# Scores of paired attention steps placed behind the values of the step ahead, and norm roots turned inside the MLP's second block

## The chip, the cores and the metric

The kernel runs on 1 core of one Trainium2 chip. The metric is the device time of an execution in microseconds, the median of the runs shown. TensorE (PE) does the matrix products, VectorE (DVE), ScalarE (ACT) and GpSimd (POOL) the rest, and SyncE (SP) issues most transfers.

## The reference

A trunk of two layers runs over 512 latent tokens and 256 context tokens, 1024 features each, in fp32. A layer is: modulated RMSNorm, one input projection whose columns go to four head groups, the groups, an output projection with a gated residual, a second modulated RMSNorm, and an MLP with squared ReLU. In the second layer the context feeds keys and values alone. What the change touches are two of the head groups and the second norm:

```python
def neighbourhood_attention(p_lat, p_ctx, rpb, need_ctx):
    ...
    s = jnp.einsum('brnqhd,brnkhd->brnhqk', qb, kb).astype(jnp.float32) * scale + bias.astype(jnp.float32)
    s = jnp.where(valid[None, None, :, None], s, NEG_INF)
    s_ctx = jnp.einsum('brnqhd,bkhd->brnhqk', qb, kc).astype(jnp.float32) * scale
    p = jax.nn.softmax(jnp.concatenate([s, s_ctx], axis=-1), axis=-1).astype(v.dtype)
    ...
def window_attention(p_lat, p_ctx, sink, ang, need_ctx):
    """Banded GQA: |i - j| <= SWA_WINDOW over latent tokens, plus all context keys and a per-head sink logit."""
    ...
    p = jax.nn.softmax(jnp.concatenate([s, s_ctx, s_sink], axis=-1), axis=-1).astype(v.dtype)
    ...
        h = h + m[5] * sq_relu_mlp(modulate(rmsnorm(h, g_norm2[l]), m[3], m[4]), w_mlp1[l], w_mlp2[l])
        if need_ctx:
            ...
            hc = hc + mc[5] * sq_relu_mlp(modulate(rmsnorm(hc, g_norm2[l]), mc[3], mc[4]), w_mlp1[l], w_mlp2[l])
```

## The kernel before

**Products.** Activations lie with features on the partitions and tokens along the row. A product of two fp32 operands is done as three products of a narrower type: each operand is split into a high and a low part (`split_w`, ScalarE's cast on L238 and VectorE's difference on L239 for weights), and `dense` (L246 to L263) runs, for one block of 128 output features, 8 products high by high, 8 low by high and 8 high by low into one PSUM bank, for the latent columns (512 wide) and then the context columns (256 wide). Its `evac` takes the result out of the bank. `dense` has a hook, `midway`, a function that is called at the middle product.

**Attention.** `attend` (L387 to L483) does one step: 128 queries of two heads. Its scores (L418 where the two heads are `paired`, L431 where not) go to PSUM banks of the pool `ps_s` (4 banks). Then VectorE takes the row maximum (L441, or L449 to L453 in steps over context keys alone), ScalarE the exponential with its sum (L455, and L458 for the sink), VectorE adds the sink (L459), takes the reciprocal (L460) and normalises (L462). TensorE transposes the probabilities (L473) into banks of the pool `ps_t` (4 banks), `evac` copies them out (ScalarE L374 or VectorE L376), and TensorE multiplies them with the values (L479). The last value product of a step is appended to the list `anchors`. In the paired branch the score products of both heads alternate and are chained by `tc.issue_after`, so that they keep that order; the first of them has no such tie.

`swa()` (L1113) runs the banded steps: 2 pairs of heads by 6 blocks of queries in layer 0 (4 latent, 2 context) and 2 by 4 in layer 1. `na()` (L1172) runs as many neighbourhood steps. `mla()` uses the unpaired branch.

**What sets the order.** Program order is only a wish here: outside the opening of layer 0, a list scheduler places the instructions of each engine by priorities and its own estimate of times, before the kernel runs. At run time each engine, TensorE too, takes its instructions in that fixed order. `tc.issue_after(x)` makes what is issued in it follow x on its engine. `merge` interleaves several chains of work: in the banded stage the steps of `swa()`, the convolution of the state-space group (`conv`, with a dense block ahead of each and four multiply-adds on VectorE, L805) and, in layer 0, splits of output weights; in the neighbourhood stage the steps of `na()`, the state-space scan and blocks of the output projection. `behind`, which `calls` uses, ties a chain's next piece to the value product two steps back (`LAG = 2`). The products of the modulation of the next use (L172 in `mod_steps`) are small pieces that are laid between.

**The norm ahead of the MLP.** `norm_seg` (L311 to L348) is a generator for one stretch of tokens: squares of 8 feature blocks, `rstd_col` (products with ones, L296, and VectorE's root, L282 to L288), `bcast` (the roots are turned to a row by products with the identity, L308), then 8 modulates (VectorE L339, then ScalarE L342/L343 or L346, and GpSimd or VectorE L347). The last stretch (context in layer 0, the second half of the latent tokens in layer 1) isn't done when the MLP begins: `rest` holds what is left of it. The MLP's first 3 blocks (5 in layer 1, `NAHEAD`) run on the first part of the tokens alone (`up_block`, L1281 to L1284 are ReLU, square and split of its result), and `next(rest)` is called in between, 6 times per block (`PACE`): in block 0 at its middle product (the roots' sums), after block 0 five times (the turn and four modulates), after block 1 the rest.

Of the kernel before, what the change touches and what calls it, by code (L numbers as in the profile page):

```python
# [59 lines left out]
PACE = (6, 6, 6)  # L60
# [31 lines left out]
def kernel(ctx: ExitStack, tc: tile.TileContext, D: dict, out: bass.AP, dbg=None):  # L92
# [4 lines left out]
    PE = nc.tensor  # L97
# [14 lines left out]
    def unit(tag, name, dtype=F32):  # L112
        if tag == "u":
            return up.tile([P, T], dtype, tag="u", name=name)
        return kp.tile([P, 776], dtype, tag=tag, name=name, bufs={"pr": 4, "pT": 3, "q": 4}[tag])

    def pss():
        return ps_s.tile([P, 512], F32, tag="s", name=nm("pS"))

    def pst():  # L120
        return ps_t.tile([P, 512], F32, tag="t", name=nm("pt"))
# [120 lines left out]
    def load_w(src, nk, low=V):  # L242
        raw = wp.tile([P, nk, P], F32, tag="wr", name=nm("wr"))
        nc.sync.dma_start(raw, src)
        return split_w(raw, [P, nk, P], wp, "wh", "wl", low=low)
# [4 lines left out]
    def dense(src, acts, segs, evac, ks=range(KD), w=None, low=V, midway=None):  # L250


        k0, nk = min(ks), max(ks) - min(ks) + 1
        wh, wl = w or load_w(src[:, k0:k0 + nk, :], nk, low)
        for s, c0, n in segs:
            ps = pst()
            mm = [(wh, 0, k) for k in ks] + [(wl, 0, k) for k in ks] + [(wh, 1, k) for k in ks]
            for i, (w, a, k) in enumerate(mm):
                if midway and i == len(mm) // 2:
                    midway()  # L260
                PE.matmul(ps[:, :n], w[:, k - k0, :], acts[k][a][:, c0:c0 + n],  # L261
                          start=i == 0, stop=i == len(mm) - 1)
            evac(s, c0, n, ps[:, :n])  # L263
        return wh, wl
# [104 lines left out]
    def evac(dst, src):  # L369

        turn[0] += turn[1]
        if turn[0] >= 1.0:
            turn[0] -= 1.0
            A.copy(dst, src)  # L374
        else:
            V.tensor_copy(dst, src)  # L376

    anchors = []
# [11 lines left out]
    def attend(q, k, parts, sinks, vt, put, sgn=-1.0, paired=False):  # L390
# [8 lines left out]
        def terms(a):  # L399
            if not isinstance(q[a], tuple):  # L400
                return [(q[a], k[a])]
            return [(q[a][0], k[a][0]), (q[a][1], k[a][0]), (q[a][0], k[a][1])]

        ats = ([], [])
        if paired:


            off, prev = 0, None
            for k0, n, tab in parts:
                if off == 0 or off + n - b0 > 512:  # L410
                    banks, b0 = (pss(), pss()), off
                dst = [banks[a][:, off - b0:off - b0 + n] for a in range(2)]
                nmm = len(terms(0))
                for i in range(nmm):
                    for a in range(2):
                        x, y = terms(a)[i]
                        with (tc.issue_after(prev.ins) if prev else nullcontext()):
                            prev = PE.matmul(dst[a], x, y[:, k0:k0 + n], start=i == 0, stop=i == nmm - 1)  # L418
                for a in range(2):
                    ats[a].append((dst[a], off, n, tab))  # L420
                off += n
        else:
            for a in range(2):
                off = 0
                for k0, n, tab in parts:
                    if off == 0 or off + n - b0 > 512:
                        bank, b0 = pss(), off
                    dst = bank[:, off - b0:off - b0 + n]
                    mm = terms(a)
                    for i, (x, y) in enumerate(mm):  # L430
                        PE.matmul(dst, x, y[:, k0:k0 + n], start=i == 0, stop=i == len(mm) - 1)  # L431
                    ats[a].append((dst, off, n, tab))
                    off += n
# [33 lines left out]
        for a in range(2):  # L467
            pT = unit("pT", nm("pT"))
            for g0 in range(0, nkt, 4):
                n = min(4, nkt - g0)  # L470
# [6 lines left out]
        for t in range(nkt):  # L477
            for a in range(2):
                last_mm = PE.matmul(pv[64 * a:64 * a + 64, :P], vt(a, t), pts[a][:, t * P:(t + 1) * P],  # L479
                                    start=t == 0, stop=t == nkt - 1)  # L480
# [139 lines left out]
    def transition(block, norm, parts):  # L620


        w, before = {}, iter(())
        for pi, part in enumerate(parts):
            order = range(KD) if pi % 2 == 0 else range(KD - 1, -1, -1)
            now = norm(*part, order)
            for i, d in enumerate(order):
                w[d] = block(d, part, w[d] if pi and i < REUSE else None)
                for _ in range(BACK[i]):
                    next(before, None)  # L630
                if i:
                    next(now)
            for _ in before:
                pass
            next(now)
            before = now
        return before

    for l in range(DEPTH):
        last = l == DEPTH - 1  # L640
# [3 lines left out]
        parts = [(0, 0, 256), (0, 256, 256)] if last else full  # L644
# [626 lines left out]
        rest = transition(lambda d, p, w: out_block(d, 1, *p, KB, w), norm2, fine)  # L1271
# [4 lines left out]
        def up_block(qd, f, sg, out=None, w=None, midway=None):  # L1276
            hh, hl = out or (unit("u", nm("hh"), F32R), unit("pT" if f == KD - 1 else "u", nm("hl"), F32R))

            def act(s, c0, n, ps):
                r, r2 = unit("q", nm("r")), unit("pr", nm("r2"))  # L1280
                A.activation(r[:, :n], ps, AF.Relu)  # L1281
                A.activation(hh[:, c0:c0 + n], r[:, :n], AF.Square)
                V.tensor_tensor(r2[:, :n], r[:, :n], r[:, :n], ALU.mult)  # L1283
                V.tensor_tensor(hl[:, c0:c0 + n], r2[:, :n], hh[:, c0:c0 + n].bitcast(F32), ALU.subtract)  # L1284

            w = dense(D["w_mlp1"][l, qd * KD + f], nacts, sg, act, w=w, low=(V, G)[LOWU[l]], midway=midway)
            return (hh, hl), w
# [12 lines left out]
        if not last:  # L1300
            sums, ahead = mod_sums(l + 1), split_ahead(l + 1)
# [3 lines left out]
        for qd in range(4):  # L1305
            hid = []
            if qd == 0:
                ahead = []
                for f in range(NAHEAD[l]):
                    ahead.append(up_block(qd, f, parts[:1], midway=None if f else lambda: next(rest)))  # L1310
                    for _ in range(PACE[l] - (f == 0)):
                        next(rest, None)
                for _ in rest:
                    pass
                for f, (o, w) in enumerate(ahead):
                    hid.append(up_block(qd, f, parts[1:], o, w if len(ahead) < 3 else None)[0])
            while len(hid) < KD:
                hid.append(up_block(qd, len(hid), segs)[0])
                more(MV[0])
            if qd < 3:  # L1320
                for d in range(KD):
                    down_block(qd, d, hid, segs)
                    more(MV[1])
# [12 lines left out]
        rest = transition(lambda d, p, w: down_block(3, d, hid, [p], w), norm1, fine)  # L1336
# [132 lines left out]
```

## Time and profile before

| | |
|---|---|
| median of 3 runs | 1802.9 us (1801.73 to 1808.01) |
| the profiled execution | 1802.71 us, its span 1800.9 us |
| granted TensorE clock, mean | 0.987 of full |
| TensorE busy | 1750.6 us, 97% of the span |
| weight loads (PEld) | 1493.3 us, 83% |
| VectorE busy | 1109.4 us, 62% |
| ScalarE busy | 737.8 us, 41% |
| GpSimd busy | 240.3 us, 13% |

A row of a timeline gives the start of an instruction (or of a run of like ones), its time, its engine, line and operation, output and inputs, and in brackets how long the engine was idle before it and what ended that. Buffer numbers are left out of names in the trace and stand in the orders below: `pS` are scores, `pr` probabilities, `pt` a bank of `ps_t`, `wh`/`wl` the parts of a weight, `ah`/`al` of an activation, `rs` norm roots, `xn`, `r`, `hl` blocks of the MLP. The layers' stages lie so in the span: banded attention 205 to 330 us and 1225 to 1300 us, neighbourhood attention with the state-space scan 330 to 465 us and 1300 to 1412 us, the start of the first MLP at about 500 us.

### The profile page before, as it was taken

The numbers are of one execution on the slowest core, as the hardware profiler recorded it, in microseconds if no ns is written. First come the engines' busy times: TensorE is split into PE (matmuls) and PEld (weight loads), VectorE is DVE, ScalarE is ACT, GpSimd is POOL, SyncE is SP. The second block draws the span as 40 slices with busy tenths as digits, with TensorE's granted clock in tenths as the row PEclk, the third lists the DMA queues.
The fourth block names the chain that finished last, engine by engine and source line by source line (L and its number), as shares of the span: only waits on it lengthen the run. The fifth ranks groups of instructions, "written<-read, shape, count | busy, mean of one in ns | idle before, by whom it ended". The sixth has DMA issues, their size and how long they took to land.

```text
span 1800.9 us, 28892 instructions
## 1 busy us (share of the span) xinstructions
PE 1750.6 (97%) x11170; PEld 1493.3 (83%) x11170; DVE 1109.4 (62%) x2372; ACT 737.8 (41%) x1497; POOL 240.3 (13%) x367
## 2 busy tenths in 40 slices
PE   8999999999989999999999999999989999999998
PEld 7877877777878888888888998688878898888888
DVE  5548458688677566467555674757779563444355
ACT  4347546655353123123123443545544451323244
POOL 0102011234320000000000331101114310000002
PEclk8999999999999999999999999899999999999999
DMA  9440267632635445344444534111333543222333
GB/s 337 138 152 17 67 214 248 214 115 93 211 109 177 136 153 163 109 154 144 155 135 146 173 113 138 35 36 36 120 110 104 199 146 100 94 94 94 106 104 119
DMA packets 86249, 238.94 MB, mean 133 GB/s; under 512 B 9200, under 2 KB 17392, under 8 KB 86112
## 3 DMA queue, kind: packets, MB, share of 16 engines
q1 hardware_dynamic: 74976, 208.57, 35.8%
q0 software_dynamic: 7104, 24.33, 3.8%
q10 hardware_dynamic: 4032, 4.20, 0.7%
q8 instruction: 88, 1.44, 0.3%
q14 instruction: 49, 0.40, 0.1%
HBM read 214.52 MB, written 22.54 MB: 132 GB/s over the span
## 4 chain that ended last, share of the span: by engine, by line
PE 89%; DVE 6%; DMA 2%; ACT 1%; issue 1%; POOL 0%; DVEq 0%; ACTq 0%; POOLq 0%; SPq 0%
PE pt L261 68%; PE pt L479 3%; PE pt L473 3%; PE pS L666 2%; PE pS L431 2%; PE pS L418 2%; PE pt L172 1%; PE pt L666 1%; PE pt L296 1%; PE pt L933 1%; PE pS L1031 1%; DVE pr L441 1%; DVE wl L239 1%; PE pt L864 0%; DMA old<-in_hT_dram 0%
## 5 line engine op out<-in xcount | busy, mean ns | idle before, releaser
L238 ACT CAST wh<-wr 128x1024 fp32r<-128x1024 f32 x206 | 215.9, 1049 | 403.0 <-PE pt L261 291.2
L239 DVE TENSOR_TENSOR wl<-wr,wh 128x1024 fp32r<-128x1024 f32 x206 | 253.9, 1233 | 100.5 <-ACT wh L238 96.0
L261 PE MATMUL pt<-ah,wh 128*128 128x512 f32 (+1 forms) x1304 | 275.0, 352 | 7.1 <-ACT ah L346 3.1
L261 PE MATMUL pt<-al,wh 128*128 128x512 f32 (+1 forms) x1304 | 269.5, 347 | 0.0
L261 PE MATMUL pt<-ah,wl 128*128 128x512 f32 (+1 forms) x1304 | 268.7, 348 | 0.0
L261 PEld LDWEIGHTS pt<-ah,wh 128*128 128x128 f32 x1304 | 213.3, 190 | 48.0 <-ACT ah L346 4.3
L261 PEld LDWEIGHTS pt<-ah,wl 128*128 128x128 f32 x1304 | 215.2, 191 | 31.4 <-issue 0.8
L261 PEld LDWEIGHTS pt<-al,wh 128*128 128x128 f32 x1304 | 212.9, 190 | 31.1 <-issue 2.4
L261 PE MATMUL pt<-hh,wh 128*128 128x256 f32 (+1 forms) x896 | 168.2, 330 | 0.0
L261 PE MATMUL pt<-hl,wh 128*128 128x256 f32 (+1 forms) x896 | 167.0, 329 | 0.0
L261 PE MATMUL pt<-hh,wl 128*128 128x256 f32 (+1 forms) x896 | 166.9, 329 | 0.0
L1291 DVE SCALAR_TENSOR_TENSOR h<-pt,mod,h 128x512 f32<-128x512 f32 (+1 forms) x112 | 66.3, 595 | 153.8 <-PE pt L261 153.6
L261 PEld LDWEIGHTS pt<-hh,wh 128*128 128x128 f32 x896 | 137.6, 189 | 17.7 <-issue 0.6
L261 PEld LDWEIGHTS pt<-hh,wl 128*128 128x128 f32 x896 | 138.0, 190 | 15.4
L261 PEld LDWEIGHTS pt<-hl,wh 128*128 128x128 f32 x896 | 138.1, 190 | 15.0
L208 DVE SCALAR_TENSOR_TENSOR ma<-wm,cact,ma 128x768 f32<-128x768 f32 x112 | 109.9, 1013 | 65.3 <-DMA wm<-in_w_mod_dram 65.2
L1281 ACT ACTIVATE r<-pt 128x512 f32<-128x512 f32 (+1 forms) x101 | 51.4, 509 | 237.1 <-PE pt L261 237.1
L1283 DVE TENSOR_TENSOR r<-r 128x512 f32<-128x512 f32 (+1 forms) x101 | 58.2, 577 | 123.0 <-ACT r L1281 122.9
L322 POOL TENSOR_TENSOR sq<-sq,sq 128x256 f32<-128x256 f32 x66 | 64.7, 980 | 442.9 <-ACT sq L318 442.2
L455 ACT ACTIVATE pr<-pr,m 128x512 f32<-128x512 f32 (+2 forms) x96 | 77.8, 811 | 40.3 <-DVE m L441 38.4
L261 PE MATMUL pt<-oh,wo 128*128 128x256 f32 (+1 forms) x576 | 93.9, 306 | 0.0
L261 PEld LDWEIGHTS pt<-oh,wo 128*128 128x128 f32 x576 | 79.0, 194 | 5.5 <-issue 1.7
(295 smaller groups left out, 2473.5 us busy)
## 6 DMA issues: line engine op xcount, KB each, us to landing
wr<-in_w_mlp_dram SPq DMA_DIRECT2D x154, 512.0 KB, 3.5
wo<-oscr SPq DMA_DIRECT2D x66, 512.0 KB, 4.7
wm<-in_w_mod_dram SPq DMA_DIRECT2D x80, 384.0 KB, 3.6
wr<-in_w_a_dram SPq DMA_DIRECT2D x36, 512.0 KB, 4.1
wm<-in_w_mod_dram SPq DMA_DIRECT2D x32, 512.0 KB, 4.0
wr<-in_w_out_dram SPq DMA_DIRECT2D x16, 512.0 KB, 4.3
oscr<-wh POOLq DMA_DIRECT2D x16, 512.0 KB, 3.7
oscr<-wl POOLq DMA_DIRECT2D x16, 512.0 KB, 5.6
```

Of the source, the lines that this page charges most:

```text
L208: V.scalar_tensor_tensor(a[:, :T], w, cact[:, k, i:i + 1], a[:, :T], ALU.mult, ALU.add)
L238: A.copy(wh, raw)
L239: low.tensor_tensor(wl, raw, wh.bitcast(F32), ALU.subtract)
L261: PE.matmul(ps[:, :n], w[:, k - k0, :], acts[k][a][:, c0:c0 + n], start=i == 0, stop=i == len(mm) - 1)
L322: G.tensor_tensor(sq[0][:, :n], sq[0][:, :n], q[:, :n], ALU.add)
L455: A.activation(pr[:, :off], src, AF.Exp, scale=-1.0 if tabs else sgn, bias=mcol, accum_out=s2[:, a:a + 1])
L473: PE.transpose(pt[:, i * P:(i + 1) * P], probs[a][:, (g0 + i) * P:(g0 + i + 1) * P], ident)
L479: last_mm = PE.matmul(pv[64 * a:64 * a + 64, :P], vt(a, t), pts[a][:, t * P:(t + 1) * P], start=t == 0, stop=t == nkt - 1)
L666: PE.matmul(acc[t], acts[k][a][:, t * P:(t + 1) * P], slabs[pc][w][:, kk, :], start=k == 0 and x == 0, stop=k == KD - 1 and x == 2)
L1281: A.activation(r[:, :n], ps, AF.Relu)
L1283: V.tensor_tensor(r2[:, :n], r[:, :n], r[:, :n], ALU.mult)
L1291: V.scalar_tensor_tensor(h[d][:, c0:c0 + n], ps, mod[:, 40 + d, s:s + 1], h[d][:, c0:c0 + n], ALU.mult, ALU.add)
```

## The change

The first score product of a paired step is now tied behind the last entry of `anchors`, the last value product of the step that was issued ahead. Before, only the later ones were tied to each other. And `midway` is now a pair, the product's number and the function: block 0 calls `next(rest)` at product 12 as before, and no more behind it; block 1 calls it at product 6 in layer 0 and 18 in layer 1, so the roots are turned there; all 8 modulates of the stretch follow, 6 after block 1 and 2 after block 2 (as `PACE` has it).

```diff
--- before.py
+++ after.py
@@ -256,8 +256,8 @@
             ps = pst()
             mm = [(wh, 0, k) for k in ks] + [(wl, 0, k) for k in ks] + [(wh, 1, k) for k in ks]
             for i, (w, a, k) in enumerate(mm):
-                if midway and i == len(mm) // 2:
-                    midway()
+                if midway and i == midway[0]:
+                    midway[1]()
                 PE.matmul(ps[:, :n], w[:, k - k0, :], acts[k][a][:, c0:c0 + n],
                           start=i == 0, stop=i == len(mm) - 1)
             evac(s, c0, n, ps[:, :n])
@@ -405,7 +405,7 @@
         if paired:
 
 
-            off, prev = 0, None
+            off, prev = 0, anchors[-1] if anchors else None
             for k0, n, tab in parts:
                 if off == 0 or off + n - b0 > 512:
                     banks, b0 = (pss(), pss()), off
@@ -414,8 +414,8 @@
                 for i in range(nmm):
                     for a in range(2):
                         x, y = terms(a)[i]
-                        with (tc.issue_after(prev.ins) if prev else nullcontext()):
-                            prev = PE.matmul(dst[a], x, y[:, k0:k0 + n], start=i == 0, stop=i == nmm - 1)
+                        with (tc.issue_after(prev) if prev else nullcontext()):
+                            prev = PE.matmul(dst[a], x, y[:, k0:k0 + n], start=i == 0, stop=i == nmm - 1).ins
                 for a in range(2):
                     ats[a].append((dst[a], off, n, tab))
                 off += n
@@ -1307,8 +1307,9 @@
             if qd == 0:
                 ahead = []
                 for f in range(NAHEAD[l]):
-                    ahead.append(up_block(qd, f, parts[:1], midway=None if f else lambda: next(rest)))
-                    for _ in range(PACE[l] - (f == 0)):
+                    now = (12, (6, 18)[last], None)[min(f, 2)]
+                    ahead.append(up_block(qd, f, parts[:1], midway=now and (now, lambda: next(rest))))
+                    for _ in range(PACE[l] if f else 0):
                         next(rest, None)
                 for _ in rest:
                     pass
```

A scheduler decides where instructions come to stand, so three places of its result follow.

TensorE, layer 0, the first banded step (its probabilities are `pr_2635` and `pr_2645`, its scores `pS_2619`, `pS_2620`, `pS_2627`, `pS_2628`). Before:

```order
L261 MATMUL pt_2561<-al_245,wh_2531 128x256
L261 MATMUL pt_2561<-al_247,wh_2531 128x256
L473 MATMUL pt_2656<-con,pr_2635 128x128 x4
L473 MATMUL pt_2662<-con,pr_2635 128x128
L172 MATMUL pt_2330<-wm_2748,cact 32x512 x2
L172 MATMUL pt_2330<-wm_2750,cact 32x512 x2
L418 MATMUL pS_2780<-oh_1726,nqh_2774 128x384
L418 MATMUL pS_2781<-oh_1726,nqh_2774 128x384
L418 MATMUL pS_2780<-oh_1726,nql_2775 128x384
```

In the change:

```order
L418 MATMUL pS_2627<-oh_1726,nqh_2613 128x256
L418 MATMUL pS_2628<-oh_1726,nqh_2613 128x256
L418 MATMUL pS_2627<-oh_1726,nql_2614 128x256
L418 MATMUL pS_2628<-oh_1726,nql_2614 128x256
L418 MATMUL pS_2627<-ol_1727,nqh_2613 128x256
L418 MATMUL pS_2628<-ol_1727,nqh_2613 128x256
L172 MATMUL pt_2330<-wm_2748,cact 32x512 x2
L172 MATMUL pt_2330<-wm_2750,cact 32x512 x2
L473 MATMUL pt_2656<-con,pr_2635 128x128 x4
L473 MATMUL pt_2662<-con,pr_2635 128x128
L473 MATMUL pt_2666<-con,pr_2645 128x128 x4
L473 MATMUL pt_2672<-con,pr_2645 128x128
```

Before, the transposes of `pr_2635` follow the last products of a dense block (`pt_2561`), and the step's last score stands 57 rows above them, ahead of that block. In the change the step's scores stand behind that block, and between the last of them and the transposes of their own probabilities only two rows of the modulation are left.

VectorE, the softmax of the same step. Before:

```order
L441 ISA pr_2635,m_559_2617<-pS_2619,con,mx_2636 128x384
L441 ISA m_559_2617 128x1
L441 ISA pr_2645,m_559_2617<-pS_2620,con,mx_2646 128x384
L441 ISA m_559_2617 128x1
L239 TENSOR_TENSOR wl_2608<-wr_2605,wh_2607 128x1024
L459 TENSOR_TENSOR s_560_2618<-s_560_2618,e_567_2640 128x1
L460 RECIPROCAL s_560_2618<-s_560_2618 128x1
L462 TENSOR_SCALAR pr_2635<-pr_2635,s_560_2618 128x640
L239 TENSOR_TENSOR wl_2693<-wr_2690,wh_2692 128x1024
L459 TENSOR_TENSOR s_560_2618<-s_560_2618,e_570_2650 128x1
L460 RECIPROCAL s_560_2618<-s_560_2618 128x1
L462 TENSOR_SCALAR pr_2645<-pr_2645,s_560_2618 128x640
```

In the change:

```order
L805 SCALAR_TENSOR_TENSOR acc_2595<-raw_2525,hconv_713,acc_2595 128x772
L441 ISA pr_2645,mx_2646<-pS_2628,zero,nsink_2458 128x256
L441 ISA mx_2646 128x1
L441 ISA pr_2635,m_559_2617<-pS_2619,con,mx_2636 128x384
L441 ISA m_559_2617 128x1
L805 SCALAR_TENSOR_TENSOR acc_2595<-raw_2525,hconv_713,acc_2595 128x772
L441 ISA pr_2645,m_559_2617<-pS_2620,con,mx_2646 128x384
L441 ISA m_559_2617 128x1
L805 SCALAR_TENSOR_TENSOR acc_2595<-raw_2525,hconv_713,acc_2595 128x772
L459 TENSOR_TENSOR s_560_2618<-s_560_2618,e_567_2640 128x1
L805 SCALAR_TENSOR_TENSOR acc_2595<-raw_2525,hconv_713,acc_2595 128x772
L460 RECIPROCAL s_560_2618<-s_560_2618 128x1
```

Before, two splits of weights (L239) stand in the chain. Now four steps of a convolution (L805) stand in it, the last of them ahead of the reciprocal, and the normalise (L462) comes two rows further down.

Layer 0's MLP, TensorE where the roots `rs_6009` are summed (L296) and turned (L308), then VectorE behind it. TensorE before:

```order
L261 MATMUL pt_5991<-al_5660,wh_5987 128x512
L261 MATMUL pt_5991<-al_5662,wh_5987 128x512
L296 MATMUL pt_6004<-ones,sq_5825 128x1 x2
L261 MATMUL pt_5991<-al_5664,wh_5987 128x512
L308 MATMUL pt_6037<-con,rs_6009 128x128 x2
L261 MATMUL pt_6066<-ah_5649,wh_6062 128x512
L261 MATMUL pt_6066<-ah_5651,wh_6062 128x512
```

VectorE before:

```order
L288 SCALAR_TENSOR_TENSOR rs_6009<-rsv_6010,rs_6009 128x2
L1284 TENSOR_TENSOR hl_5984<-r_1322_6032,hh_5983 128x512
L339 SCALAR_TENSOR_TENSOR xn_6040<-h_3902,gsc_96,pt_6037 128x256
L339 SCALAR_TENSOR_TENSOR xn_6045<-h_4019,gsc_96,pt_6037 128x256
L339 SCALAR_TENSOR_TENSOR xn_6049<-h_4131,gsc_96,pt_6037 128x256
L339 SCALAR_TENSOR_TENSOR xn_6053<-h_4239,gsc_96,pt_6037 128x256
```

TensorE in the change, from the last products of the next latent block on:

```order
L261 MATMUL pt_6045<-al_5660,wh_6041 128x512
L261 MATMUL pt_6045<-al_5662,wh_6041 128x512
L261 MATMUL pt_6045<-al_5664,wh_6041 128x512
L308 MATMUL pt_6052<-con,rs_6009 128x128 x2
L261 MATMUL pt_6113<-ah_5649,wh_6109 128x512
L261 MATMUL pt_6113<-ah_5651,wh_6109 128x512
```

VectorE in the change:

```order
L288 SCALAR_TENSOR_TENSOR rs_6009<-rsv_6010,rs_6009 128x2
L1283 TENSOR_TENSOR r_1322_6032<-r_6031 128x512
L239 TENSOR_TENSOR wl_6156<-wr_6153,wh_6155 128x1024
L1284 TENSOR_TENSOR hl_5984<-r_1322_6032,hh_5983 128x512
L1283 TENSOR_TENSOR r_1331_6074<-r_6073 128x512
L339 SCALAR_TENSOR_TENSOR xn_6079<-h_3902,gsc_96,pt_6052 128x256
L339 SCALAR_TENSOR_TENSOR xn_6084<-h_4019,gsc_96,pt_6052 128x256
L339 SCALAR_TENSOR_TENSOR xn_6088<-h_4131,gsc_96,pt_6052 128x256
L239 TENSOR_TENSOR wl_6193<-wr_6190,wh_6192 128x1024
L1284 TENSOR_TENSOR hl_6038<-r_1331_6074,hh_6037 128x512
```

The turn (L308) moves from behind block 0 to behind a whole further block (`pt_6045`), and the context's modulates (L339) from behind the roots to behind `r_1331_6074`, the squared result of that further block.

## Rows read from the trace of the kernel before

**Rows 1.** the page: engines (section 1) and chain of waits (section 4)

```profile
PE 1750.6 (97%) x11170; PEld 1493.3 (83%) x11170; DVE 1109.4 (62%) x2372; ACT 737.8 (41%) x1497; POOL 240.3 (13%) x367
...
PE 89%; DVE 6%; DMA 2%; ACT 1%; issue 1%; POOL 0%; DVEq 0%; ACTq 0%; POOLq 0%; SPq 0%
```

**Rows 2.** TensorE's waits: waited for, us in total, times, longest us

```profile
PE pt L308 <- DVE rs L288: 8.6, 4, 3.0
...
PE pt L473 <- DVE pr L462: 0.4, 1, 0.4
```

**Rows 3.** windows: stages, busy us of each engine, granted clock, DMA share, GB/s

```profile
205.00:330.00 125.00, 121.53 (x835) 95.19 (x831) 82.73 (x190) 68.21 (x149) 17.47 (x40) 1.00 0.59 194
330.00:465.00 135.00, 125.80 (x1022) 101.25 (x1022) 105.14 (x350) 73.03 (x205) 47.38 (x70) 0.99 0.40 134
1225.00:1300.00 75.00, 75.00 (x514) 61.30 (x514) 55.51 (x132) 38.75 (x86) 8.75 (x27) 1.00 0.21 68
1300.00:1412.00 112.00, 103.56 (x904) 89.77 (x901) 88.31 (x293) 51.13 (x133) 30.80 (x46) 0.98 0.42 139
```

**Rows 4.** TensorE's timeline, a banded step: start us, us, what, [idle <-releaser]

```profile
241.34 0.50 PE L418 MATMUL pS<-ol,nqh 64*128 64x256 f32 x2
...
251.81 0.71 PE L473 MATMUL pt<-con,pr 128*128 128x128 f32 x5
252.45 1.06 PE L172 MATMUL pt<-wm,cact 128*32 128x512 f32 x8
```

**Rows 5.** VectorE's timeline of the same step

```profile
241.76 0.48 DVE L441 CUSTOM_DVE_ANT_0 pr<-pS,zero,nsink 128x256 f32<-128x256 f32 x1 [3.60 <-PE pS L418]
...
243.65 1.22 DVE L239 TENSOR_TENSOR wl<-wr,wh 128x1024 fp32r<-128x1024 f32 x1
244.79 0.16 DVE L459 TENSOR_TENSOR s<-s,e 128x1 f32<-128x1 f32 x1
...
245.18 0.55 DVE L462 TENSOR_SCALAR pr<-pr,s 128x640 f32<-128x640 f32 x1
```

**Rows 6.** groups by line and shape, VectorE, 205 to 465 us

```profile
L805 DVE SCALAR_TENSOR_TENSOR acc<-raw,hconv,acc 128x772 f32<-128x772 f32 x24 | 24.4, 1017 | 0.5 <-ACT acc L803 0.4
L239 DVE TENSOR_TENSOR wl<-wr,wh 128x1024 fp32r<-128x1024 f32 x17 | 20.8, 1223 | 14.9 <-ACT wh L238 12.2 <-issue 2.5 <-DMA oscr<-wl 0.2
```

**Rows 7.** ScalarE's timeline of the same step

```profile
243.24 0.83 ACT L455 ACTIVATE pr<-pr,m 128x640 f32<-128x640 f32 x1
```

**Rows 8.** TensorE's timeline, layer 0's first MLP blocks

```profile
512.83 0.50 PE L296 MATMUL pt<-ones,sq 128*128 128x1 f32 x4
...
516.68 0.43 PE L308 MATMUL pt<-con,rs 128*128 128x128 f32 x2 [3.01 <-DVE rs L288]
516.87 3.18 PE L261 MATMUL pt<-ah,wh 128*128 128x512 f32 x8
...
529.47 3.01 PE L261 MATMUL pt<-ah,wh 128*128 128x256 f32 x22
...
538.31 2.00 PE L261 MATMUL pt<-ah,wh 128*128 128x512 f32 x8
```

**Rows 9.** TensorE's timeline, end of the neighbourhood stage of layer 0

```profile
462.17 0.40 PE L308 MATMUL pt<-con,rs 128*128 128x128 f32 x2 [2.73 <-DVE rs L288]
```

**Rows 10.** windows of 4 us behind two waits, columns as in rows 3

```profile
464.00:468.00 4.00, 4.00 (x27) 4.00 (x27) 1.34 (x3) 0.00 (x0) 0.00 (x0) 0.71 0.37 126
516.00:520.00 4.00, 3.32 (x11) 2.64 (x12) 3.89 (x9) 2.23 (x6) 0.85 (x1) 0.69 0.41 131
520.00:524.00 4.00, 4.00 (x17) 3.27 (x16) 0.15 (x1) 0.20 (x1) 0.73 (x1) 0.88 0.00 0
```

**Rows 11.** VectorE's timeline, context modulates of layer 0's MLP, first and last

```profile
517.23 1.66 DVE L339 SCALAR_TENSOR_TENSOR xn<-h,gsc,pt 128x256 f32<-128x256 f32 x4
...
533.17 0.48 DVE L347 SCALAR_TENSOR_TENSOR al<-xn,mod,ah 128x256 fp32r<-128x256 f32 x1
```

**Rows 12.** TensorE's timeline, the same turn of norm roots in layer 1

```profile
1437.67 0.63 PE L308 MATMUL pt<-con,rs 128*128 128x128 f32 x2
```

## Prediction

> **What bounds the kernel now.** I read four things, in this order. The page's engine shares and the chain of waits: TensorE is busy 97% of the span and carries 89% of the chain [rows 1], so a time on TensorE's queue is a time of the kernel, and room to gain is small while room to lose is wide. Then TensorE's waits: the longest are for norm roots, 3.0 us at most, and the transposes of probabilities (L473) wait for a normalised row (L462) once, for 0.4 us [rows 2]. So in the kernel before softmax costs TensorE next to nothing in all 40 paired steps (12 banded and 12 neighbourhood steps in layer 0, 8 and 8 in layer 1). Third, the stages: the two banded stages (205 to 330 and 1225 to 1300 us) and the two neighbourhood stages keep TensorE busy for 425.89 of 447 us, 21.1 us idle [rows 3]. Fourth, one banded step closely, for why the wait is hidden: its last scores start at 241.34, VectorE begins on them at 241.76 and starts the first normalise at 245.18, and TensorE meets its transposes only at 251.81, after values and a whole dense block [rows 4, 5]. Ten us of products cover a chain of four.
>
> **Part 1, the scores behind the values.** It removes and adds no work; it pins the first score of a paired step behind the last values of the step ahead. On SP two loads of output weights (wo) change places with one or two neighbours; that they come earlier or a place later I take as nothing, since the neighbourhood stages have idle time to cover it [rows 3]. The order of TensorE shows the cost: the step's dense block now stands ahead of its scores, and between scores and transposes only four products of the modulation (L172) are left, in other banded steps nothing, in neighbourhood steps 0 to 5 us. The next dense block can't fill in, as it stands behind those transposes. So TensorE waits in each step for max, exponential, sum, root and normalise.
>
> How long, I worked out from rows. For the step shown, VectorE's order from first max to first normalise holds four maxes, four convolution steps (L805), two sums, one root, and the normalise. The four maxes take 243.65 − 241.76 = 1.89 us [rows 5]; an L805 is 1.02 us long [rows 6], and its end lies 0.08 over the next start, as that of every instruction on this engine, so 0.94; the two sums and the root 0.2 each, the normalise 0.47 without such an end [rows 5]. That is 1.89 + 3.76 + 0.6 + 0.47 = 6.7 us; less the 1.0 us of L172 (1.06 with its tail) [rows 4] it is 5.7 us of wait. The same for all 40 steps (VectorE's instructions that stand in the chain in the new order, by their row durations, less TensorE's work that stands between) gives 45.8 us for the 12 banded steps of layer 0 (1.1 to 6.7 each), 36.5 for the 8 of layer 1, 13.2 for the 12 neighbourhood steps of layer 0 (six of them about nothing) and 22.9 for the 8 of layer 1: 118.4 us. Not in it is the time in which VectorE itself waits for the exponential, 0.83 us [rows 7] and its hand-over: 1.1 us in each of 20 banded steps, 0.8 in 14 neighbourhood steps, 33 us. **Taken: +151.6 us.** Bounds: 118 if every exponential hides behind an L805 or a split, 76 if the fillers also run elsewhere (second rival); above, a weight split of 1.22 us [rows 6] more in each of 32 steps, 190.
>
> Against it stands idle time of before that the new waits absorb: of the 21.1 us [rows 3] part is SSD's and stays. I take −13, between 0 and −21. Paired scores that no longer stand alone are in it.
>
> **The clock.** After the 3.01 us wait at 516.68 the granted clock was 0.69 and 0.88 in the two slices of 4 us behind it; after the 2.73 us wait at 462.17 it was 0.71 in the slice 464 to 468 [rows 8 to 10]. Between the two levels, 1.2 and 2.4 GHz, 0.69 and 0.88 are 2.5 and 1.0 us at the lower one, so 3.4 us at half speed: 1.7 us lost for one wait. Of the 40 new waits 32 are over 2.2 us. All of them at 1.7 is 54; the other end is 0. No row of before shows waits in a series, so I take 1.15 each, nearer the rows than zero: **+37 us.** The Trainium skill ("TensorE: Matmul & The Clock Gate", section "HAM oscillation — how this bites in real kernels") tells of a kernel that waits once per round of its loop and pays the lower clock anew in each, 1.67 us at half rate; an estimate by that figure is 40 × 0.83 = 33 us, and this sum would come out 4 us lower.
>
> **Part 2, the norm roots.** In layer 0 TensorE waits 3.01 us for the roots (L288) before it turns them (L308) [rows 8]. Now a block of latent products stands between sums and turn: 24 of 128x512. Before, 48 of them took 516.87 to 529.47, 12.6 us with the 1.7 lost to the clock, so 24 are 5.5 us, and the chain from sums to turned roots (512.83 to 516.68, 3.9 us) fits in [rows 8]. That takes away 3.0 us and the 1.7 us of clock, −4.7. But the turn comes a block later, and the eight context modulates behind it too. Before, they ran from 517.23 to 533.65 [rows 11], beside 12.6 us of latent products and then the context products (529.47 to 538.31) [rows 8]. Now only 24 latent products, 5.5 us, stand ahead of the first context product, which wants the tiles one by one, and on VectorE the modulates queue behind a squared block (r_1331) that itself waits for the last of these products. Followed by hand with those durations, the four late tiles cost waits of 1.4, 2.0, 2.2 and 1.5 us, and the block ends about 541.0 instead of 538.3, and with one more dip of clock **+3 us**; bounds −4.7 (all of it hidden) and +5. On SP the modulation weights (wm) keep their place. In layer 1 the turn had no wait before (1437.67) [rows 12], and there is nothing to win: 0 to +3, in the same +3.
>
> **Sum.** 1802.7 (the profiled execution, 0.2 under the median shown, so the two are one here) + 151.6 − 13 + 37 + 3 = **1981 us**. The next thing late on each new wait is the dense block behind it, and with it the convolution's input; these are on the path already and are not counted twice.
>
> **The rivals.**
> - *Only the clean chain shows.* If VectorE's fillers fall in TensorE's own waits of other places, a step costs the bare chain: 241.76 to 245.73 (normalise of 0.55 at 245.18), 4.0 us [rows 5], less 1.0 of L172, 2.9 × 20 = 58; half the neighbourhood sum, 18; a third of the clock, 13. 1802.7 + 58 + 18 − 13 + 13 + 3 = 1882. For it: VectorE is no bound over a stage. Against it: its order is fixed, and the L805 stand inside the chain.
> - *The clock stays down through the stages.* With a wait in each step, TensorE may run at the lower level for half of the banded stages: their 196.5 us of work [rows 3] then take 98 more, in place of 37: 2042. For it: both long waits of before were followed by it. Against it: full clock was back within 8 us both times [rows 8, 10]. The section of the skill named above speaks for a toll in every round, not for a clock that stays down.
> - *The waits hide after all.* Where the chain from first max to normalise were no longer than TensorE's work between (1.0 us in the banded steps), part 1 costs nothing, part 2 gives its 4.7 and 3 us of the idle time go: 1795, faster. For it: before, transposes hardly ever waited [rows 2]. Against it: the bare chain is 4.0 us, four times that point.
> - *The order changes nothing that shows*, as other queues release TensorE: 1803.
>
> **How the numbers follow.** Forecast 0.64, clean chain 0.14, low clock 0.16, hidden 0.04, nothing 0.02. About 0.5%, 9 us, is what a measurement of this kernel can tell from no change. Faster is the hidden case, 0.04; within 0.5% the last, 0.02; slower all others, 0.94. The forecast's own range is 1895 (118 of waits, 21 of idle back, no clock, −4.7) to 2035 (190, 54, +5 and 17 of idle back). With the clean chain below, less some of its clock, and the low clock above, 1870 to 2050 holds 8 in 10.
>
> **What would show it.** In TensorE's waits of the changed kernel, L473 waiting for L462 should lead, with about 40 waits and 120 to 190 us; the two banded stages should be 110 us longer together and the neighbourhood stages 45, with granted clock under 0.95 in the banded ones. L308's longest wait in layer 0's MLP should be under 0.5 us, and waits of the first context products for modulated tiles (L346, L343) should stand in its place, 4 to 9 us. It is wrong if L473 waits under 60 us in all, if stages outside these four change by over 10 us, or if the clock in them stays at 1.00.

## The result, and the profile after

The changed kernel takes 2014.2 us (median of 4 runs, 2011.88 to 2016.33) against 1803.7 for the kernel before: 1.1163 times, 95% interval 1.1139 to 1.1187. The forecast was 1981, inside 1870 to 2050. The profiled execution has a span of 2011.9 us, 211 more than before, and a mean granted clock of 0.936 against 0.987.

The page of the changed kernel, its engine shares and its chain of waits, answers to [rows 1]:

```profile
PE 1816.3 (90%) x11170; PEld 1541.8 (77%) x11170; DVE 1113.3 (55%) x2372; ACT 747.8 (37%) x1497; POOL 235.5 (12%) x367
...
PE 81%; DVE 12%; ACT 3%; DMA 3%; issue 1%; POOL 0%; SPq 0%; ACTq 0%; DVEq 0%; POOLq 0%
```

TensorE was idle 1800.9 − 1750.6 = 50.3 us before and is idle 2011.9 − 1816.3 = 195.6 now: **145.3 us more idle**. And it is busy **65.7 us longer** with the same 11170 products, which goes with the lower clock. The two are the whole difference, and part of the chain has moved from TensorE (89% before, 81% now) to VectorE and ScalarE.

TensorE's waits (what it waited for, us in total, times, the longest), where [rows 2] had one wait of 0.4 us in the first of these lines:

```profile
PE pt L473 <- DVE pr L462: 59.1, 26, 6.7
PE pt L473 <- DVE s L460: 50.9, 7, 9.2
PE pt L473 <- ACT pr L464: 19.0, 6, 6.2
PE pt L473 <- ACT e L458: 8.5, 2, 4.2
...
PE pt L473 <- DVE s L459: 5.0, 1, 5.0
```

All five are one thing, a transpose (L473) that waits for its step's probabilities; the releaser named is only what came last by the profile. With two smaller lines they are 145.6 us, against 151.6 forecast. There are 45 of them, 27 at 2 us and more.

The stages, as in [rows 3], with moved boundaries. They are not the same work window by window: the banded windows now hold more products (1018 where 835 were, 659 where 514 were), and the last one ends at a place that lay at 1432.81 before, not at 1412:

```profile
206.00:437.00 231.00, 166.32 (x1018) 130.82 (x1015) 97.46 (x231) 86.99 (x199) 21.37 (x52) 0.82 0.38 130
437.00:573.45 136.45, 112.11 (x824) 87.17 (x822) 90.13 (x303) 60.23 (x154) 40.00 (x58) 0.90 0.27 90
1338.70:1495.00 156.30, 110.78 (x659) 89.74 (x655) 68.29 (x171) 51.09 (x114) 9.33 (x29) 0.79 0.17 56
1495.00:1642.24 147.24, 114.09 (x880) 99.40 (x880) 91.98 (x291) 53.05 (x128) 40.90 (x55) 0.89 0.32 108
```

Granted clock is 0.82 and 0.79 in the banded stages and 0.90 and 0.89 in the neighbourhood stages; before it was 1.00 in the former, 0.99 and 0.98 in the latter. Between equal places of the program, both stages of layer 0 together take 110 us longer (206 to 573.45, before 205 to 462.17), and both of layer 1 96 us (1338.70 to 1627.53, before 1225 to 1418.07).

The step that the prediction worked out, where [rows 4] had the transposes ten us behind the scores (it is the second banded step of layer 0; the section on the change calls it the first). TensorE's timeline:

```profile
258.50 1.06 PE L172 MATMUL pt<-wm,cact 128*32 128x512 f32 x8
268.79 2.15 PE L473 MATMUL pt<-con,pr 128*128 128x128 f32 x9 [9.22 <-DVE s L460]
```

VectorE's timeline of the same step:

```profile
261.01 1.23 DVE L239 TENSOR_TENSOR wl<-wr,wh 128x1024 fp32r<-128x1024 f32 x1 [3.06 <-ACT wh L238]
262.15 0.48 DVE L441 CUSTOM_DVE_ANT_0 pr<-pS,zero,nsink 128x256 f32<-128x256 f32 x1
...
266.96 1.02 DVE L805 SCALAR_TENSOR_TENSOR acc<-raw,hconv,acc 128x772 f32<-128x772 f32 x1
267.90 0.15 DVE L460 RECIPROCAL s<-s 128x1 f32<-128x1 f32 x1
...
268.09 0.55 DVE L462 TENSOR_SCALAR pr<-pr,s 128x640 f32<-128x640 f32 x1
```

TensorE ends the last work it has at 259.56 and waits 9.22 us. From the first max (262.15) to the end of the first normalise (268.64) VectorE takes 6.5 us, 6.7 by the row sum of the prediction, with the convolution's L805 in it. But it begins 3 to 4 us late: ahead of the maxes in its order stands a weight split (L239) that waits for ScalarE's cast of the same weight, and ScalarE's row says for what that cast waits:

```profile
259.94 1.04 ACT L238 CAST wh<-wr 128x1024 fp32r<-128x1024 f32 x1 [4.68 <-DMA wr<-in_w_a_dram]
```

A transfer of weights. Where TensorE wants the probabilities at once, whatever stands ahead of the first max counts, even a wait for a weight that nobody needs yet.

Layer 0's MLP, TensorE's timeline, which answers to [rows 8]:

```profile
622.74 0.50 PE L296 MATMUL pt<-ones,sq 128*128 128x1 f32 x4
...
628.91 0.38 PE L308 MATMUL pt<-con,rs 128*128 128x128 f32 x2
...
634.58 0.87 PE L261 MATMUL pt<-ah,wh 128*128 128x256 f32 x6
636.42 0.62 PE L261 MATMUL pt<-ah,wh 128*128 128x256 f32 x3 [0.97 <-ACT wh L238]
638.44 2.29 PE L261 MATMUL pt<-ah,wh 128*128 128x256 f32 x9 [1.40 <-ACT ah L343]
642.24 1.01 PE L261 MATMUL pt<-ah,wh 128*128 128x256 f32 x3 [1.50 <-ACT ah L343]
643.99 0.58 PE L261 MATMUL pt<-ah,wh 128*128 128x256 f32 x1 [0.74 <-ACT ah L346]
```

The turn (L308 at 628.91) now has no wait. The late modulates put four waits, 0.97 + 1.40 + 1.50 + 0.74 = 4.6 us, into the first context products instead.

### The profile page after: what moved, and what is told of

It reads as the page before. It is cut to its first block, busy times and chain, and to the rows that moved or that the text cites. A ratio compares the mean times of both kernels' runs of the same rounds, so it can differ in the third digit from the quotient of the medians.

```text
span 2011.9 us, 28931 instructions
## 1 busy us (share of the span) xinstructions
PE 1816.3 (90%) x11170; PEld 1541.8 (77%) x11170; DVE 1113.3 (55%) x2372; ACT 747.8 (37%) x1497; POOL 235.5 (12%) x367
## 4 chain that ended last, share of the span: by engine, by line
PE 81%; DVE 12%; ACT 3%; DMA 3%; issue 1%; POOL 0%; SPq 0%; ACTq 0%; DVEq 0%; POOLq 0%
PE pt L261 62%; PE pt L479 4%; PE pt L473 4%; PE pS L666 2%; DVE pr L441 2%; PE pS L431 2%; DVE acc L805 2%; PE pS L418 1%; DVE wl L239 1%; PE pt L666 1%; PE pt L296 1%; DVE pr L462 1%; ACT pr L455 1%; PE pt L933 1%; PE pt L172 1%
## 5 line engine op out<-in xcount | busy, mean ns | idle before, releaser
L239 DVE TENSOR_TENSOR wl<-wr,wh 128x1024 fp32r<-128x1024 f32 x206 | 254.0, 1234 | 126.5 <-ACT wh L238 112.7
L261 PE MATMUL pt<-ah,wh 128*128 128x512 f32 (+1 forms) x1304 | 291.2, 366 | 10.2 <-ACT ah L343 5.2
L261 PEld LDWEIGHTS pt<-ah,wh 128*128 128x128 f32 x1304 | 225.1, 200 | 55.6 <-ACT ah L343 6.6
L473 PE MATMUL pt<-con,pr 128*128 128x128 f32 x512 | 98.2, 341 | 145.8 <-DVE pr L462 59.1
L473 PEld LDWEIGHTS pt<-con,pr 128*128 128x128 f32 x512 | 73.6, 174 | 166.8 <-issue 91.8
L1281 ACT ACTIVATE r<-pt 128x512 f32<-128x512 f32 (+1 forms) x101 | 51.4, 509 | 239.8 <-PE pt L261 239.8
L261 PE MATMUL pt<-oh,wo 128*128 128x256 f32 (+1 forms) x576 | 99.0, 317 | 0.0
```

The lines of the kernel that those rows point to most:

```text
L239: low.tensor_tensor(wl, raw, wh.bitcast(F32), ALU.subtract)
L473: PE.transpose(pt[:, i * P:(i + 1) * P], probs[a][:, (g0 + i) * P:(g0 + i + 1) * P], ident)
```

## The experiments

### One part and one stage at a time

The first run has the change's scores alone, and the MLP as before:

```diff
-                    now = (12, (6, 18)[last], None)[min(f, 2)]
-                    ahead.append(up_block(qd, f, parts[:1], midway=now and (now, lambda: next(rest))))
-                    for _ in range(PACE[l] if f else 0):
+                    ahead.append(up_block(qd, f, parts[:1], midway=None if f else (12, lambda: next(rest))))
+                    for _ in range(PACE[l] - (f == 0)):
```

> The first part of the change alone; the MLP's norm roots are turned where the kernel before turns them. Theory (the parts add, and part 2 costs the 2.5 us that the MLP's start is longer by in layer 0 and some 1.5 in layer 1): 2010 us, ratio to before 1.114; TensorE's waits at L473 about 145 us in all, granted clock 0.936. Rival (part 2's late tiles carry more than that, since they follow the long waits): 2000 us or less.

Measured: 2008.3 us, ratio 1.1129 (1.1111 to 1.1148), idle 196.1 us, busy 1809.6. The first part is nearly all of the change.

The next two tie one kind of step only, which the sink tells apart (the second has `is None`):

```diff
-            off, prev = 0, anchors[-1] if anchors else None
+            off, prev = 0, anchors[-1] if anchors and sinks is not None else None
```

> Only the banded steps (those with a sink) are tied behind the values of the step ahead; part 2 is undone. Theory: the waits of the 20 banded steps as in the changed kernel, 107 us, and their clock, some 45 us, less 7 us of idle time that was there: 1948 us. Rival (the waits of one stage are given back in the next, since the state-space group's inputs are ready earlier there): 1925 us or less.

> Only the neighbourhood steps are tied; part 2 is undone. Theory: waits of 36 us, clock some 14, less 5 us idle that was there: 1848 us; together with the banded half the two differences make that of the first part alone, within 10 us. Rival (the halves overlap, the clock is lost once for a stage and not per wait): the two differences exceed it by over 20 us.

Measured: banded 1948.4 us (1.0796, interval 1.0775 to 1.0818), as expected; neighbourhood 1865.1 us (1.0335, 1.0312 to 1.0359), 17 above. The differences to the 1805.0 of the kernel before beside them are 143.4 and 60.1, together 203.5, and both together (scores_only) 203.2: they add, and nothing of one stage is given back in the other. The pages, banded first, show how each divides:

```profile
PE 1793.9 (92%) x11170; PEld 1524.9 (78%) x11170; DVE 1114.0 (57%) x2372; ACT 742.5 (38%) x1497; POOL 234.4 (12%) x367
```

```profile
PE 1776.6 (95%) x11170; PEld 1510.6 (81%) x11170; DVE 1108.9 (59%) x2372; ACT 742.8 (40%) x1497; POOL 237.8 (13%) x367
```

With spans of 1946.2 and 1866.7 us that is, banded, 43.3 us of longer busy time and 102.0 of idle more than before; neighbourhood, 26.0 and 39.8. The neighbourhood half came out over its expectation in both, 14 and 31 expected.

### How far back the tie goes

```diff
-            off, prev = 0, anchors[-1] if anchors else None
+            off, prev = 0, anchors[-2] if len(anchors) > 1 else None
```

> The changed kernel with the first score tied behind the values two steps ahead instead of one. By its order a dense block stands again between a step's scores and its transposes in most steps; the sums of VectorE's chain less TensorE's work give 13 us of wait in place of 118. Theory (what costs is the cover, not the tie): 1803 + 13 + 4 of part 2 and a little clock, 1815 to 1825 us. Rival (any tie that keeps scores from moving up costs most of it): over 1900 us.

Measured: 1852.1 us, ratio 1.0268 (1.0245 to 1.0291). The theory holds in kind, some 160 of the 211 us are back, but its number was 30 us too low. TensorE's waits of this kernel:

```profile
PE pt L473 <- DVE pr L462: 10.0, 8, 3.7
PE pt L479 <- ACT pT L374: 8.5, 7, 2.9
...
PE pt L473 <- DVE s L460: 5.5, 3, 2.7
...
PE pt L479 <- DVE pT L376: 1.9, 1, 1.9
```

The L473 lines come to 17.7 us, near the 13 of the sums. What the sums left out are the values (L479), which wait 10.4 us for the copies of the transposed probabilities, further small waits (idle is 79.2 us in all, 28.9 over before), and 18.1 us of slower products.

### What stands in the softmax chain

Four of five convolution steps are left out, in the changed kernel and in the kernel before:

```diff
-            for kk in range(1, 5):
+            for kk in range(1, 1):
```

> The changed kernel with four of the five convolution steps left out (the multiply-adds L805 on VectorE), so that the convolution has its first weight alone. Theory (the four of them stand inside the softmax chain of ten banded steps): the waits at L473 fall by 24 us by the row sums, and some clock with them: 1980 us, and the longest waits go from 7 to 9 us to 4 or 5. Rival (VectorE would do them in time it has anyway): 2008 us or more.

> The kernel before with the same four convolution steps left out. Theory (there they run beside products and bound nothing): 1800 to 1804 us. Rival (VectorE's load sets the banded stages in both kernels): 1785 us or less.

Measured: changed kernel 1996.9 us (1.1077, 1.1056 to 1.1099), 17 less than with them; kernel before 1799.5 (0.9976, 0.9965 to 0.9987), 4 less. TensorE's waits of the changed one without them:

```profile
PE pt L473 <- DVE pr L462: 82.0, 30, 6.2
PE pt L473 <- ACT pr L464: 17.6, 8, 4.4
PE pt L473 <- DVE s L459: 13.2, 3, 4.9
PE pt L473 <- ACT e L458: 8.4, 2, 4.2
```

With the smaller lines the L473 waits fall from 145.6 to 123.4, by 22 us where the sum said 24: the L805 did stand in the chain, and in the kernel before they cost 4 us in all. But the rest of the expectation failed: the time is 1996.9 us and not 1980, the longest wait 6.2 and not 4 to 5, and no clock came with it: busy time is 1819.8 us, not below the 1816.3 of the changed kernel. There are still 27 waits of 2 us and more. Shorter waits did not cost less clock.

### Work in the place of the wait

Score products of 128x512, their result unused, follow the scores of each banded step in the changed kernel, `n` of them, 16 in one run and 24 in the other:

```diff
+        if paired and sinks is not None:
+            pf = pst()
+            for i in range(n):
+                with tc.issue_after(prev):
+                    prev = PE.matmul(pf[:, :512], terms(0)[0][0], terms(0)[0][1][:, 0:512], start=True, stop=True).ins
```

> The changed kernel with 16 score products of 128x512 more in each banded step, laid between the step's scores and its transposes; their result is not used. They are 16 x 0.227 = 3.6 us of work in a place where TensorE waits 2.1 to 9.2 us. Theory (the second cost of a wait is the lower clock on the products behind it): TensorE's idle time falls by about 70 us, the granted clock of the banded stages comes back to over 0.95, and the time falls by 35 to 50 us although work is added: about 1970 us. Rival (TensorE is slow there for another cause, as contention with VectorE and ScalarE for the banks): no gain, 2014 to 2020 us, granted clock under 0.85 in the stages.

Measured: 2003.8 us, ratio 1.1103 (1.1082 to 1.1124). Idle fell by 64 us as expected, but time by 10, not 35 to 50. The third banded step of the three kernels shows why. In the changed kernel its transposes waited 6.13 us, until 290.34, and the granted clock in slices of 4 us was:

```profile
288.00:292.00 4.00, 1.30 (x5) 0.93 (x5) 3.79 (x9) 3.47 (x8) 0.56 (x1) 0.50 0.19 77
292.00:296.00 4.00, 3.69 (x12) 3.14 (x13) 1.79 (x4) 0.48 (x3) 0.72 (x4) 0.50 0.94 301
296.00:300.00 4.00, 4.00 (x21) 3.02 (x21) 0.74 (x1) 1.05 (x1) 0.00 (x0) 0.90 0.21 81
```

With 16 products (L438; the transposes are L478 in this kernel), TensorE's timeline and the same kind of slices:

```profile
279.46 3.89 PE L438 MATMUL pt<-oh,nqh 64*128 64x512 f32 x16
...
286.96 2.37 PE L478 MATMUL pt<-con,pr 128*128 128x128 f32 x10 [2.61 <-DVE s L465]
```

```profile
284.00:288.00 4.00, 1.39 (x9) 1.07 (x6) 3.96 (x10) 2.59 (x8) 0.45 (x1) 0.74 0.62 207
288.00:292.00 4.00, 4.00 (x14) 3.40 (x13) 2.33 (x4) 1.97 (x4) 0.55 (x1) 0.50 0.15 62
292.00:296.00 4.00, 4.00 (x21) 3.00 (x22) 0.00 (x0) 0.00 (x0) 0.73 (x4) 0.90 0.90 306
```

The wait is 2.61 us instead of 6.13, and the clock falls just the same: 0.50 behind it, 0.90 in the third slice.

> As the run with 16 unused score products per banded step, now with 24, 5.4 us each. With 16 the waits that stayed in the banded stages were mostly 2.4 to 3.2 us, and the granted clock still fell to 0.50 behind them. Theory (the toll of the clock is per wait, much the same for one of 2.4 us and one of 9, and goes only where the wait itself goes): the waits left are under 1.5 us in most steps, the clock comes back, TensorE's work grows by 36 us of added products less 15 to 20 of clock, idle falls by 20: 1995 to 2003 us, granted clock 0.97. Rival (it falls with these stages' own products, not with the waits): 2015 us or more, granted clock as with 16, 0.956.

Measured: 2008.8 us, ratio 1.1133 (1.1117 to 1.1149), between the two expectations, as is the granted clock of the profiled execution, 0.962. The same step with 24:

```profile
287.33 1.63 PE L478 MATMUL pt<-con,pr 128*128 128x128 f32 x10 [0.67 <-ACT raw L812]
```

```profile
284.00:288.00 4.00, 3.33 (x22) 1.70 (x20) 3.96 (x11) 3.04 (x9) 0.50 (x1) 1.00 0.11 14
288.00:292.00 4.00, 3.99 (x20) 3.17 (x20) 1.38 (x3) 1.02 (x3) 0.00 (x0) 1.00 0.71 248
292.00:296.00 4.00, 4.00 (x34) 3.10 (x33) 1.22 (x1) 1.32 (x2) 1.28 (x5) 1.00 0.42 131
```

With a wait of 0.67 us the clock stays at 1.00. Over the banded stage of layer 0 (240 to 436 us in slices of 4) it is full in 41 of 49 slices, in the changed kernel in 18. So in this stage the clock went with the waits and not with the stage's products, and at this step a wait of 2.61 us cost as much of it as one of 6.13. The runs do not tell the shorter wait from the added products as the reason, since both came together. In layer 1 four waits of 1.66 to 2.70 us were left in the banded steps, and the clock was at the lower level behind each of them. One unused product is 3.89 / 16 = 0.24 us; 320 and 480 of them are 77 and 115 us of work, TensorE is busy 51.4 and 83.3 us longer, so 26 and 32 us of clock came back. But the time did not follow, as work that fills a wait costs what the wait did, and more where the wait was shorter. What the expected 1995 to 2003 had wrong is the clock: the step from 16 to 24 products added 38 us of work and took away 21.5 us of idle time, as expected, but gave back some 6 us of clock where 15 to 20 were expected.

### The norm roots by themselves

The second part of the change alone (the scores as before), and the same with four latent blocks ahead in layer 0, the second pair of lines:

```diff
-            off, prev = 0, anchors[-1] if anchors else None
+            off, prev = 0, None
...
-NAHEAD = (3, 5)
+NAHEAD = (4, 5)
```

> The second part of the change alone: roots turned in the MLP's second block, scores as before. Theory (the wait of 3.0 us goes, the eight modulates come too late for the first context products): 2 to 5 us slower, 1807 us, ratio 1.002. Rival (the wait and its clock are won and the late tiles are hidden): 1799 us, ratio 0.997.

> The second part alone, and in layer 0 four latent blocks ahead of the context in place of three, so that 48 products instead of 24 stand between the turn of the roots and the first context product; one weight slab more is loaded and split twice. Theory (late tiles were the price): their waits of 4 to 7 us go and the gain shows, 1799 us, ratio 0.998. Rival (the reload and its split cost as much, or the tiles wait for something else): 1804 us or more.

And the kernel before with the second pair of lines alone:

> The kernel before with four latent blocks ahead of the context in layer 0 and nothing of the change. Theory (the gain of the run with both comes from the hidden turn of the roots): the wait of 3.0 us stays, 1802 to 1805 us, ratio 0.999 to 1.001. Rival (the fourth block alone brings it): 1799 us, ratio 0.998 or less.

Measured: the second part alone 0.24% slower (ratio 1.0024, 1.0011 to 1.0036), about 4 us; with four blocks ahead 0.26% faster than the kernel before (0.9974, 0.9965 to 0.9983), 1798.9 us; the four blocks alone 1.0009 (1.0000 to 1.0018). So it takes both. TensorE's timeline with the second part alone:

```profile
517.72 0.38 PE L308 MATMUL pt<-con,rs 128*128 128x128 f32 x2
...
523.39 0.87 PE L261 MATMUL pt<-ah,wh 128*128 128x256 f32 x6
525.23 0.62 PE L261 MATMUL pt<-ah,wh 128*128 128x256 f32 x3 [0.97 <-ACT wh L238]
527.25 2.27 PE L261 MATMUL pt<-ah,wh 128*128 128x256 f32 x9 [1.40 <-ACT ah L343]
```

and with four blocks ahead:

```profile
519.76 0.38 PE L308 MATMUL pt<-con,rs 128*128 128x128 f32 x2
...
530.88 1.96 PE L261 MATMUL pt<-ah,wh 128*128 128x256 f32 x15
532.67 1.12 PE L261 MATMUL pt<-ah,wl 128*128 128x256 f32 x8
```

In the first the context products (128x256) begin 5.7 us behind the turn and wait for a weight's cast, then tile by tile (two more such waits follow). In the second they begin 11.1 us behind it and run through.

The last run is that with four blocks, with layer 1 as before:

```diff
-                    now = (12, (6, 18)[last], None)[min(f, 2)]
+                    now = (12, None if last else 6, None)[min(f, 2)]
...
-                    for _ in range(PACE[l] if f else 0):
+                    for _ in range(PACE[l] - (f == 0) if last else PACE[l] if f else 0):
```

> Roots turned in the second block and four latent blocks ahead in layer 0 only; layer 1 as in the kernel before, where the turn had no wait and where the second part of the change brought a new one of 1.2 us. Theory: 1 to 2 us better than with the change in both layers, ratio to before 0.9965. Rival (the new wait in layer 1 hides a later one): the same, 0.9974.

Measured: 0.9985 (0.9972 to 0.9998). It is not the 0.9965 expected, and not told apart from the 0.9974 of the run with both layers: the wait of 1.2 us in layer 1 is worth too little to be seen.

## Why the prediction was right

**The main step was right.** The softmax chain of each paired step, hidden before, stands in TensorE's way, and with the tie two steps back most of the cost is gone. *Taken: +151.6 us of waits, −13 of idle that was there*, 139: idle rose by 145.3, the second part's share in it. The L473 lines are 145.6: 63.7 and 44.7 in the banded steps of the two layers, where the sums with the exponential said 59.0 and 45.3, and 37.2 in the neighbourhood steps, where they said 47.3. With one stage tied alone idle rose by 102.0 and 39.8 us. The waits were fewer and longer than the prediction's 32 of over 2.2 us: there are 25. And its reading of [rows 2], one wait of 0.4 us at L473, left out a second of 0.9 (for the reciprocal, L460), which changes nothing in the sum. Within the banded steps the second was 9.2 us instead of 5.7 + 1.1, by the weight split that stood ahead of its maxes and waited for a transfer: what precedes the chain on its engine belongs into the sum as well.

**The fillers in the chain** (L805) were right by 22 us against 24.

**The mis-sized term is the clock:** *"I take 1.15 each, nearer the rows than zero: +37 us"*. Measured is 65.7 us of longer busy time, 29 more, of the 33 us between 1981 and 2014. Shared out over the waits at L473 of 2 us and more it is 2.4 us each: 65.7 / 27 in the changed kernel, 43.3 / 18 with the banded tie alone, 69.2 / 27 without the convolution steps (65.8 / 27 against the kernel before without them). It is no price for one wait, though: with the neighbourhood tie alone the same division gives 26.0 / 7 = 3.7, and with the tie two steps back 18.1 / 3 = 6.0. Shorter waits cost clock too: behind one of 1.96 us at L473, until 482.66 in the changed kernel, it was 0.57 and 0.58 from 484 to 492, and behind those of 1.40 and 1.50 us in the MLP 0.52, 0.50 and 0.70 from 638 to 650. The rows of before had given 1.7 for a wait of 3 us [rows 8 to 10], and I marked them down for no reason that a row gave. The runs say the other way: behind the 6.13 us wait the products ran at the lower level from 290.34 to past 296, about 2.5 us lost (5.0 us of work in the first two slices shown at 0.50). Nor does the loss grow with the wait. Three more slices of the changed kernel:

```profile
264.00:268.00 4.00, 0.00 (x0) 0.00 (x0) 4.00 (x10) 2.21 (x6) 0.00 (x0) 0.50 0.90 348
268.00:272.00 4.00, 3.00 (x12) 2.53 (x13) 3.35 (x8) 3.10 (x6) 1.11 (x2) 0.50 0.20 78
1488.00:1492.00 4.00, 3.39 (x18) 2.43 (x20) 1.25 (x4) 1.59 (x5) 0.00 (x0) 0.51 0.02 6
```

In the wait of 9.22 us, until 268.79, the clock fell while TensorE still had nothing to do; the products behind it lost 1.5 us in the second slice and, at 0.88, 0.5 in the next. Those behind a wait of 2.76 us, until 1488.50, lost 1.7 us in the third and, at 0.64, 1.4 in the next. The Trainium skill ("TensorE: Matmul & The Clock Gate", section "HAM oscillation — how this bites in real kernels") has the toll in every round of a loop, and so it is here; its size in that section, half of 1.67 us, is a third of the 2.4 that the changed kernel shows.

**The low-clock rival** (2042) came nearer to the measured 2014 than the forecast's own 1981, by 28 us against 33, so the number alone doesn't speak for the forecast. What does is the mechanism: full clock came back between most steps, in 18 of the 49 slices, and the banded half lost 43.3 us to the clock, nearer to the 23 of 20 waits at 1.15 than to the rival's 98.

**The signs** named ahead came in the main: L473 leads the waits, the clock is below 0.95 in the banded stages, the turn's wait in the MLP is gone, and 4.6 us of waits for tiles and a weight stand in its place, 3.6 of them for tiles. One was too small: *110 us* for the banded and *45* for the neighbourhood stages. The runs with one kind of step tied give 143 and 60; the two signs make 155 together, where the prediction's own sum adds 176 for these stages.

**The second part** (+3) was right in sign and mechanism: 4.3 us by the ratio of the run by itself, with four waits of 4.7 us in place of the four of 7.1 that were followed by hand; the first of them was for a weight's cast and not for a tile. The gain of the hidden turn was real, as the run with a fourth block shows.

**Stages outside** did as foreseen: from the end of the context's first products (652.13) to the same place in layer 1 (1260.06) the kernel takes 607.9 us, 608.0 before.

## What to carry to other kernels

Before tying an instruction behind another for the sake of order, look at what then stands between it and its first consumer on the same in-order engine: that is the cover, and here it went from ten us of products to one. A wait on TensorE costs itself and a toll of clock on the products behind it, which in the changed kernel came to 2.4 us for each wait of 2 us and more and did not grow with the wait; that speaks for few long waits rather than many middling ones; work that only filled the waits won back 10 us of 211 at best. And moving a step later to hide a wait (the turned roots) needs as much cover behind it as it took in front: it paid only with one more independent block.

## What the runs showed of the hardware

The lower clock's cost did not grow with a wait's length: waits of 6.13 and 2.61 us at the same step were followed by the same slices of 0.50 and 0.90, and one of 0.67 us by none. I had expected it to shrink with the wait. In a long wait part of the time at the lower clock fell into the wait itself, where it cost nothing. And a wait that stands ahead of a chain on another engine counted in full: whether the transfers' share of the late start (a cast waiting 4.68 us for its weight) could be taken away by another order was not tried.
